# Two-layer hybrid decoder trunk: a table load, weight copies, turns and the last row's factors in another order

## The chip, the cores and the metric

The kernel runs on one core of a Trainium2 chip. The metric is the time of one execution on the device, in microseconds (us). Five engines work side by side, each through its own instructions in order: TensorE (PE in the profile; its weight loads are PEld), VectorE (DVE), ScalarE (ACT), GpSimd (POOL) and SyncE (SP), which issues most DMA transfers. They wait for each other by semaphores.

## The reference

The input is 512 tokens of 1024 channels in fp32. Two layers each do `h = h + mixer(rms_norm(h))` and then `h = h + ffn(rms_norm(h))`; a last RMSNorm gives the output.

```
# layer 0: gated short convolution beside causal pooling
proj = xn @ w_in_even                        # 1024 -> 4 x 512: a_b, a_c, a_v, z
y_a  = a_b * causal_dwconv3(a_c * a_v, conv_a)
y_b  = (causal_pool(z) @ w_pool) * pool_scale
h    = h + concat(y_a, y_b) @ w_out_even
# layer 1: chunked spatial gating
u, v = split(gelu(xn @ w_in_odd))            # 1024 -> 2 x 1024
vn   = rms_norm(v, sgu_norm)                 # chunks of 128 positions
gate = tril(w_spatial) @ vn + b_spatial
h    = h + (u * gate) @ w_out_odd
# both layers
g    = causal_dwconv3(hn @ w_gate, conv_ffn) + b_conv
h    = h + (silu(g) * (hn @ w_up)) @ w_down  # 2816 hidden
```

## The kernel before

The program is written in the order of the data: `mixer0`, `ffn0`, `mixer1`, `ffn1`. A scheduler then orders each engine's instructions by its own estimate, unless the text holds them in program order (`inorder`) or puts one behind another (`behind`). Activations are kept transposed, as eight tiles `h0` to `h7` of 128 channels by 512 tokens, up to the last projection.

**Precision.** A product in fp32 is made of three TensorE matmuls, on a high and a low part of each operand (`mm3`, L152). The high part is a ScalarE copy (`whi`, `hgh`, `a_hi`). The low part is a VectorE difference (`wlo`, `hgl`, `a_lo`), or, in `summed` (L135), a negated copy to which a DMA of GpSimd's queue adds the raw weight. Weights come through four buffers of 512 KB (`raw`), loaded on SyncE's queue; a load waits until the readers of the buffer's last content are done.

**Banks.** `mm_bank` hands out seven PSUM banks. A bank is free again when its reader (a copy, an addition) is done.

**Products by seven.** The feed-forward blocks, the v and u halves of mixer 1 and the last projection multiply 2 x 2 blocks by seven products in place of eight. The products use three kinds of banks (`BANK`, L529): products 1, 6, 7 and 4 all use bank "a" in turn, 5 and 3 use "e", 2 uses "b". So the copy of product 1 out of its bank goes before product 6, and the copy of 6 before 7.

**Norms.** A norm's factor is a root on ScalarE, which needs the table of its function loaded (`ACT_TABLE_LOAD`), a reciprocal and two corrections on VectorE (`newton`, L236). In mixer 0 the root is `sd_m0c`, the first root of the program; the copies of the input weights `ac` stand behind it on ScalarE.

**Feed-forward.** `steps` (L787) goes through 22 hidden tiles by groups: group 0 directly, groups 2, 4, ... by the seven products. `STEPS` (L522) tells for each group which half projection follows it and whether the rows it made are split into acts (`a_hi`, `a_lo`) behind it. `direct` (L604) runs group 0 of a feed-forward block: eight steps `i` of four sums `j` (`gu`), each step three matmuls per sum. In layer 1 a hook, `before` (L1097), puts a turn ahead of each of the first eight of these: `turn_residual` turns the residual by four TensorE transposes into a bank (`hT`), which ScalarE copies to `y`. On ScalarE the splits `t23` and `t41` of `block_sums` (L634) stand among these copies.

**Mixer 1.** `InProducts` (L896) holds one half of the input projection: `plain` makes the weights of products 1 and 2, `rest` the other five, in the order 5, 6, 7, 4, 3, and `run` the products, for two halves of the tokens (`i`). For v, `v1` is made by `plain`, `rest` and `run`. For u, `u0` is made by `plain`; then come the sums of squares of v, their root (`rv`), the normed v of the first half (`v_normed(0)`), then `rest` and `run`.

**The end.** The last projection runs product by product, with its order held by hand. For a row tile t, `taken` adds a product to `y`, `squared` makes a sum of squares, `halved` adds it up, `rooted` takes the root, `inverted` makes the factor in three VectorE instructions, `times` multiplies by the norm's gain, and `scaled` multiplies by the factor and issues the store. Row tile 3 ends before row tile 1, whose last sum comes in two parts, `c` and `d`.

Of the kernel before, what the change touches and what calls it, by code (L numbers as in the profile page):

```python
# [8 lines left out]
F32 = mybir.dt.float32  # L9
F32R = mybir.dt.float32r  # L10
BF16 = mybir.dt.bfloat16
AF = mybir.ActivationFunctionType
ALU = mybir.AluOpType
PSUM = bass.MemoryType.PSUM

P = 128
# [3 lines left out]
NT = S // P  # L20
# [7 lines left out]
LINE = 64  # L28
# [3 lines left out]
def tile_trunk(ctx: ExitStack, tc: tile.TileContext, x, norm_mix, norm_ffn, final_norm,  # L32
# [3 lines left out]
    nc = tc.nc  # L36
# [5 lines left out]
    tp = ctx.enter_context(tc.tile_pool(name="tp", bufs=2))  # L42
# [3 lines left out]
    def mm_bank(name):  # L46
        return ps_mm.tile([P, 512], F32, tag="mm", name=name)
# [40 lines left out]

    eps = small[:, 1:2]
    nc.gpsimd.memset(eps, EPS)  # L90
    inv_pos = small[:, PAD : 2 * PAD]
    for t in range(PAD):
        nc.gpsimd.memset(inv_pos[:, t : t + 1], 1.0 / (t + 1))
# [151 lines left out]
    def inv_sqrt(r, ss, n, name):  # L245

        ms = work("ms", n, name)
        nc.vector.tensor_scalar(ms, ss, 1.0 / D, EPS, op0=ALU.mult, op1=ALU.add)
        newton(ms, n, name, r)
        nc.vector.scalar_tensor_tensor(r, ms, 1.5, r, op0=ALU.add, op1=ALU.mult)  # L250

    def inv_sqrt_cols(ss, n, name):
        r = tp.tile([P, LINE], F32, tag="rc", name=f"rc_{name}")[:, :n]
        inv_sqrt(r, ss, n, name)
        return r
# [263 lines left out]

    STEPS = [(0, None, True), (2, (0, 2, 0), True), (4, (0, 2, 1), True)]  # L522
    for f in range(6, NF, 4):
        STEPS += [(f, (f - 4, f, 0), False), (f + 2, (f - 4, f, 1), f + 4 < NF)]
    HALF = S // 2
# [27 lines left out]
    class Ffn:  # L553
# [233 lines left out]
        def steps(self, half_down, before=lambda i, j: None):  # L787

            rows = []
            for f, part, ready in STEPS:  # L790
                rows += self.hidden(f, before)
# [29 lines left out]
    def mixer1(norm):  # L821
        w = w_in_odd[0]
        with tc.tile_pool(name="m1", bufs=1) as mp:
# [28 lines left out]
            ssv = mp.tile([P, 4, PAD], F32, name="ssv")[:, :, :NT]  # L852

            def v_square(half, t):
                sq = tp.tile([P, S], F32, tag="sq", name=f"sqv{half}_{t}")
                nc.scalar.activation(sq, v[t][:, half * 512 : (half + 1) * 512], AF.Square,
                                     accum_out=ssv[:, half, t : t + 1])
# [38 lines left out]
            class InProducts:  # L896
# [28 lines left out]
                    self.put(4, parts, (1, 0))  # L925
                    self.put(3, parts, (1, 1))

                def run(self, out_, done):
                    banks = ({}, {})
                    e = {}  # L930
                    for i, product in ((0, 1), (1, 1), (0, 2), (1, 2), (0, 6), (1, 6), (0, 5),
                                       (0, 7), (1, 5), (1, 7), (0, 4), (0, 3), (1, 4), (1, 3)):
                        hi, lo = self.stat[product]
                        ps = multiply(banks[i], f"{self.name}_{i}", product, tokens(product, i),
                                      lambda kp: (hi[:, kp, :], lo[:, kp, :]))
                        c = {1: (0, 0), 2: (0, 0), 6: (0, 1), 3: (0, 1), 7: (1, 1), 5: (1, 1),
                             4: (1, 0)}[product]
                        dst = out_(i + 2 * c[0])[:, c[1] * HALF : (c[1] + 1) * HALF]
                        if product in (1, 6):
                            nc.scalar.copy(dst, ps)  # L940
                        elif product == 5:
                            e[i] = ps
                        elif product == 7:
                            nc.scalar.copy(dst, ps)
                            nc.vector.tensor_tensor(dst, e[i], dst, ALU.add)
                            gelu(dst, dst, i + 2)
                        elif product == 4:
                            gelu(dst, ps, i + 2)
                            done(i + 2)
                        else:  # L950
                            nc.vector.tensor_tensor(dst, ps, dst, ALU.add)
                        if product == 3:
                            row = out_(i)
                            gelu(row, row, i)
                            done(i)

            def gelu(dst, src, t):
                nc.scalar.activation(dst, src, AF.Gelu, scale=norm.cols[:, t : t + 1])
# [3 lines left out]
            v = [mp.tile([P, D], F32, tag="v", bufs=4, name=f"v{t}") for t in range(NT)]  # L962
# [2 lines left out]
                v_square(0, t)  # L965
            v1 = InProducts("v1", 1536)
            v1.plain()
            v1.rest()
            v1.run(lambda t: v[t][:, 512:], lambda t: v_square(1, t))
            u0 = InProducts("u0", 0)  # L970
            u0.plain()

            nc.vector.tensor_tensor(ssv[:, 0, :], ssv[:, 0, :], ssv[:, 1, :], ALU.add)
            rv = inv_sqrt_cols(ssv[:, 0, :], NT, "v")
            vn = []

            def v_normed(half):
                hi = mp.tile([P, NT, S], F32R, tag="vn", bufs=4, name=f"vnh{half}")
                lo = mp.tile([P, NT, S], F32R, tag="vn", bufs=4, name=f"vnl{half}")
                for t in range(NT):  # L980
                    src = v[t][:, half * 512 : (half + 1) * 512]
                    nc.scalar.activation(hi[:, t, :], src, AF.Copy, scale=rv[:, t : t + 1])
                    nc.vector.scalar_tensor_tensor(lo[:, t, :], src, rv[:, t : t + 1],
                                                   hi[:, t, :].bitcast(F32),
                                                   op0=ALU.mult, op1=ALU.subtract)
                vn.append((hi, lo))

            v_normed(0)

            u, gt, mix = {}, {}, {}  # L990

# [32 lines left out]
                mix[j] = hi, lo  # L1024

            u[0] = mp.tile([P, NT, S], F32, tag="u", bufs=2, name="u0")
            u0.rest()
            u0.run(lambda t: u[0][:, t, :], lambda t: None)

            v_normed(1)  # L1030
            ws = wp.tile([P, NK, P], F32, tag="raw", bufs=4, name="ws")
            nc.scalar.dma_start(ws, w_spatial[0].rearrange("h t s -> t h s"))
# [46 lines left out]
    def ffn1(norm):  # L1079
        with tc.tile_pool(name="f1", bufs=1) as ap:  # L1080
# [9 lines left out]
            def turn_residual(t, half):  # L1090
                ps = mm_bank(f"hT{t}_{half}")
                for i in range(4):
                    nc.tensor.transpose(ps[:, i * P : (i + 1) * P],
                                        h[half * 4 + i][:, t * P : (t + 1) * P], ident)
                nc.scalar.copy(y[t][:, half * 512 : (half + 1) * 512], ps)

            def before(i, j):  # L1097
                if i < 2:
                    turn_residual(j, i)

            left, right = slice(0, 512), slice(512, D)

# [106 lines left out]
            vec, act, pool = nc.vector, nc.scalar, nc.gpsimd  # L1209
# [9 lines left out]
            def squared(t, cs):  # L1219
                sq = tp.tile([P, S], F32, tag="sq", name=f"sqf{t}_{cs.start}")  # L1220
                inorder(act.activation(sq[:, : cs.stop - cs.start], y[t][:, cs], AF.Square,
                                       accum_out=ssf[:, t, cs.start // 256 : cs.start // 256 + 1]))

            def halved(t, cs, first):

                ss, ms = ssf[:, t, cs.start // 256 : cs.start // 256 + 1], ssf[:, t, 3:4]
                inorder(vec.tensor_scalar(ms, ss, -0.5 / D, -0.5 * EPS if first else ms,
                                          op0=ALU.mult, op1=ALU.add))

            def rooted(t):  # L1230
                inorder(act.activation(root[t], ssf[:, t, 3:4], AF.Sqrt, scale=-2.0))

            def inverted(t):
                ms, r = ssf[:, t, 3:4], factor[t]
                inorder(vec.reciprocal(r, root[t]))
                inorder(vec.tensor_scalar(ms, ms, r, r, op0=ALU.mult, op1=ALU.mult))
                inorder(vec.tensor_scalar(r, ms, 1.5, r, op0=ALU.add, op1=ALU.mult))
# [4 lines left out]
            def scaled(engine, t, cs, queue=nc.sync):  # L1242
                dst, src, r = y[t][:, cs], rows_f[t][:, cs], factor[t]
                inorder(act.activation(dst, src, AF.Copy, scale=r) if engine is act else
                        engine.tensor_scalar(dst, src, r, None, op0=ALU.mult))
                queue.dma_start(out[t * P : (t + 1) * P, cs], dst)
# [43 lines left out]
            squared(1, right)  # L1290

            taken(2, 1, slice(0, 256), "c")
            inverted(3)
            taken(2, 1, slice(256, 512), "d")
            squared(1, left)
            halved(1, right, True)
            scaled(vec, 3, left)
            scaled(pool, 3, right)
            halved(1, left, False)
            rooted(1)  # L1300
            inverted(1)
            scaled(act, 1, right, nc.scalar)
            inorder(vec.scalar_tensor_tensor(y[1][:, left], y[1][:, left], factor[1],
# [37 lines left out]
```

## Time and profile before

| | us |
|---|---|
| three runs | 988.18, 988.68, 987.76 (median 988.18) |
| the profiled execution, own time | 987.73 |
| its span, first to last instruction | 986.0 |
| mean granted TensorE clock in it | 0.998 of full |

A row of the timeline gives the start (us from the span's start), the duration, the engine, the line, the operation, the tiles as out<-in (buffer numbers left out) and their shapes, and xN where N equal ones follow each other; in that case the duration is from the first's start to the last's end. In brackets stands how long the engine was idle before it, and what released it. Matmuls overlap: the next starts before the one before it has ended, and their ends are modelled.

### The profile page before, as it was taken

What the parts mean: (1) busy time and instruction counts of PE and PEld (TensorE: products, weight loads), DVE (VectorE), ACT (ScalarE), POOL (GpSimd) and SP (SyncE); (2) the same over time, 40 slices, a digit from 0 to 9 for tenths busy, and PEclk for the clock granted to TensorE, in tenths of its full rate; (3) what the DMA queues carried; (4) which work ended last, traced back from release to release, by engine and by line L of the source; (5) the groups of instructions that cost most, each with busy time, mean ns of one, the idle gap of its engine ahead of it and who ended that gap; (6) DMA issues with size and microseconds to landing.
All of it is one profiled execution on the core that took longest, in us unless ns stands there. A gap on an engine that the chain in (4) does not pass through costs nothing.

```text
span 986.0 us, 15484 instructions
## 1 busy us (share of the span) xinstructions
PE 974.6 (99%) x6099; PEld 879.9 (89%) x6099; DVE 772.8 (78%) x1179; ACT 560.8 (57%) x840; POOL 115.1 (12%) x131
## 2 busy tenths in 40 slices
PE   9999999999999999999999999999999999999996
PEld 6788888999999999999889988889999999999995
DVE  6897458998788887886887765579987779777787
ACT  5623347755465654655487734576655456554675
POOL 2142022000000000000210001210000000000023
PEclk9999999999999999999999999999999999999999
DMA  7442225555565454643423623165554555455674
GB/s 248 131 150 85 86 86 128 137 143 150 129 151 135 130 142 129 150 129 109 127 63 113 196 78 104 54 142 129 150 160 132 137 136 146 127 132 145 151 151 126
DMA packets 87941, 129.32 MB, mean 131 GB/s; under 512 B 4308, under 2 KB 57788, under 8 KB 87868
## 3 DMA queue, kind: packets, MB, share of 16 engines
q1 hardware_dynamic: 78172, 98.69, 32.3%
q0 software_dynamic: 8208, 27.79, 15.6%
q10 hardware_dynamic: 1488, 1.84, 0.7%
q8 instruction: 48, 0.79, 0.3%
q14 instruction: 25, 0.20, 0.1%
HBM read 98.42 MB, written 2.10 MB: 102 GB/s over the span
## 4 chain that ended last, share of the span: by engine, by line
PE 86%; DVE 7%; ACT 3%; issue 2%; DMA 1%; POOL 0%; ACTq 0%; DVEq 0%
PE dn L154 3%; PE dn L153 3%; PE dn L155 3%; PE d L154 3%; PE d L153 3%; PE d L155 3%; PE oo L155 1%; PE oo L154 1%; PE oo L153 1%; PE oe L155 1%; PE oe L154 1%; PE oe L153 1%; PE u_20a L542 1%; PE u_16a L542 1%; PE u_14a L542 1%
## 5 line engine op out<-in xcount | busy, mean ns | idle before, releaser
L576 DVE SCALAR_TENSOR_TENSOR c<-rows,prm,c 128x512 f32<-128x512 f32 x88 | 64.0, 745 | 1.5 <-ACT c L574 1.4
L140 POOL DMA_DIRECT2D wlo_g<-raw_g x20 | 17.2, 859 | 387.4 <-ACT wlo_g L139 350.4
L153 PE MATMUL d<-a_hi,whi_d 128*128 128x512 f32 x144 | 56.1, 390 | 0.0
L153 PE MATMUL dn<-whi_dn,a_hi 128*128 128x512 f32 x144 | 56.1, 390 | 0.0
L154 PE MATMUL d<-a_lo,whi_d 128*128 128x512 f32 x144 | 56.1, 390 | 0.0
L154 PE MATMUL dn<-wlo_dn,a_hi 128*128 128x512 f32 x144 | 56.1, 390 | 0.0
L155 PE MATMUL d<-a_hi,wlo_d 128*128 128x512 f32 x144 | 56.0, 389 | 0.0
L155 PE MATMUL dn<-whi_dn,a_lo 128*128 128x512 f32 x144 | 56.0, 389 | 0.0
L679 DVE TENSOR_TENSOR wlo_s34u<-s34u,whi_s34u 128x1024 fp32r<-128x1024 f32 x20 | 24.5, 1224 | 25.5 <-ACT whi_s34u L678 25.5
L149 DVE TENSOR_TENSOR wlo_dn<-raw_dn,whi_dn 128x1024 fp32r<-128x1024 f32 x18 | 22.0, 1224 | 23.6 <-ACT whi_dn L148 23.4
L142 ACT ACTIVATE whi_u<-raw_u 128x1024 fp32r<-128x1024 f32 x21 | 22.2, 1055 | 31.7 <-PE d L154 17.6
L149 DVE TENSOR_TENSOR wlo_d<-raw_d,whi_d 128x1024 fp32r<-128x1024 f32 x18 | 22.0, 1223 | 19.5 <-ACT whi_d L148 19.5
L198 ACT ACTIVATE hgh<-h,prm 128x512 fp32r<-128x512 f32 x24 | 17.3, 722 | 35.1 <-DVE h L309 35.0
L140 POOL DMA_DIRECT2D wlo_u<-raw_u x21 | 18.1, 861 | 162.0 <-ACT wlo_u L139 89.5
L584 ACT ACTIVATE s<-c,prm 128x512 f32<-128x512 f32 x44 | 31.2, 713 | 7.3 <-DVE c L576 7.2
L209 POOL TENSOR_TENSOR ssq_f<-ssq_f,sq_f 128x512 f32<-128x512 f32 x14 | 19.7, 1410 | 131.2 <-ACT sq_f L208 96.3
L260 ACT ACTIVATE a_hi<-s 128x512 fp32r<-128x512 f32 x40 | 25.0, 626 | 15.7 <-PE dn L154 9.9
L199 DVE SCALAR_TENSOR_TENSOR hgl<-h,prm,hgh 128x512 fp32r<-128x512 f32 x24 | 23.1, 964 | 12.0 <-ACT hgh L198 11.9
L155 PEld LDWEIGHTS d<-a_hi,wlo_d 128*128 128x128 f32 x144 | 27.0, 188 | 5.7
L155 PEld LDWEIGHTS dn<-whi_dn,a_lo 128*128 128x128 f32 x144 | 27.0, 188 | 5.6
L1104 DVE SCALAR_TENSOR_TENSOR y<-dn,small,y 128x512 f32<-128x512 f32 x40 | 27.7, 746 | 5.5 <-PE dn L155 5.5
L153 PEld LDWEIGHTS d<-a_hi,whi_d 128*128 128x128 f32 x144 | 27.1, 188 | 5.4
(1489 smaller groups left out, 3759.2 us busy)
## 6 DMA issues: line engine op xcount, KB each, us to landing
raw_g<-in_w_ffn_gate_dram SPq DMA_DIRECT2D x40, 512.0 KB, 3.8
raw_u<-in_w_ffn_up_dram SPq DMA_DIRECT2D x40, 512.0 KB, 3.7
raw_dn<-in_w_ffn_down_dram SPq DMA_DIRECT2D x22, 512.0 KB, 3.5
wlo_u<-raw_u POOLq DMA_DIRECT2D x21, 512.0 KB, 5.6
wlo_g<-raw_g POOLq DMA_DIRECT2D x20, 512.0 KB, 4.6
raw_d<-in_w_ffn_down_dram SPq DMA_DIRECT2D x18, 512.0 KB, 3.8
raw_oe<-in_w_out_even_dram SPq DMA_DIRECT2D x8, 512.0 KB, 3.5
raw_v<-in_w_in_odd_dram SPq DMA_DIRECT2D x8, 512.0 KB, 4.7
```

Source lines behind the costliest of these rows:

```text
L140: nc.gpsimd.dma_start(lo, raw, accum_op=ALU.add)
L149: behind(nc.vector.tensor_tensor(lo, raw, hi.bitcast(F32), ALU.subtract), after[0])
L153: nc.tensor.matmul(ps, lhs[0], rhs[0], start=start, stop=False)
L154: nc.tensor.matmul(ps, lhs[0], rhs[1], start=False, stop=False)
L155: nc.tensor.matmul(ps, lhs[1], rhs[0], start=False, stop=stop)
L199: nc.vector.scalar_tensor_tensor(hg[k][1], h[k], g, hg[k][0].bitcast(F32), op0=ALU.mult, op1=ALU.subtract)
L260: nc.scalar.activation(hi, src, AF.Copy, scale=scale)
L542: nc.tensor.matmul(ps, l, r, start=first, stop=end, skip_group_check=True)
L576: nc.vector.scalar_tensor_tensor(c, t[:, i : S + i], prm("cf", i * NF + ft), c, op0=ALU.mult, op1=ALU.add)
L584: nc.scalar.activation(s, c, AF.Silu, bias=self.prm("bf", ft))
L679: nc.vector.tensor_tensor(lo, src, hi.bitcast(F32), ALU.subtract)
L1104: return nc.vector.scalar_tensor_tensor(dst, ps, ffn.cols[:, t : t + 1], dst, op0=ALU.mult, op1=ALU.add)
```

## The change

Six edits. `sd_0` is a one-element root, issued at the program's start. `STEPS` no longer splits the rows of group 2 behind group 2; they are split together with those of group 4 (both layers). `run` takes a function that it calls behind the two products 1, ahead of product 2: for v1 that is `rest`; for u0 it is a new `beside_u0`, with the root of v, the first normed v and `rest`, which stood ahead of `run`. `before` issues the turns two at a time, ahead of every second sum. At the end, row 3's factor stands behind the last sum and its square; its right half is scaled by VectorE in place of GpSimd, behind the root of row 1.

```diff
     nc.gpsimd.memset(eps, EPS)
+    nc.scalar.activation(tp.tile([P, LINE], F32, tag="sd", bufs=1, name="sd_0")[:, :1], eps, AF.Sqrt)
...
-    STEPS = [(0, None, True), (2, (0, 2, 0), True), (4, (0, 2, 1), True)]
+    STEPS = [(0, None, True), (2, (0, 2, 0), False), (4, (0, 2, 1), True)]
...
-                def run(self, out_, done):
+                def run(self, out_, done, behind_first):
...
                     for i, product in ((0, 1), (1, 1), (0, 2), (1, 2), (0, 6), (1, 6), (0, 5),
                                        (0, 7), (1, 5), (1, 7), (0, 4), (0, 3), (1, 4), (1, 3)):
+                        if (i, product) == (0, 2):
+                            behind_first()
...
-            v1.rest()
-            v1.run(lambda t: v[t][:, 512:], lambda t: v_square(1, t))
+            v1.run(lambda t: v[t][:, 512:], lambda t: v_square(1, t), v1.rest)
             u0 = InProducts("u0", 0)
             u0.plain()
-            nc.vector.tensor_tensor(ssv[:, 0, :], ssv[:, 0, :], ssv[:, 1, :], ALU.add)
-            rv = inv_sqrt_cols(ssv[:, 0, :], NT, "v")
...
-            v_normed(0)
...
-            u0.rest()
-            u0.run(lambda t: u[0][:, t, :], lambda t: None)
+
+            def beside_u0():
+                nc.vector.tensor_tensor(ssv[:, 0, :], ssv[:, 0, :], ssv[:, 1, :], ALU.add)
+                rv.append(inv_sqrt_cols(ssv[:, 0, :], NT, "v"))
+                v_normed(0)
+                u0.rest()
+
+            u0.run(lambda t: u[0][:, t, :], lambda t: None, beside_u0)
...
             def before(i, j):
-                if i < 2:
+                if i < 2 and j % 2 == 0:
                     turn_residual(j, i)
+                    turn_residual(j + 1, i)
...
             taken(2, 1, slice(0, 256), "c")
-            inverted(3)
             taken(2, 1, slice(256, 512), "d")
             squared(1, left)
+            inverted(3)
             halved(1, right, True)
             scaled(vec, 3, left)
-            scaled(pool, 3, right)
             halved(1, left, False)
             rooted(1)
+            scaled(vec, 3, right)
             inverted(1)
             scaled(act, 1, right, nc.scalar)
```

More of the change, by code (lines that the diff above doesn't have):

```diff
@@ L967, in mixer1 @@
             v1.plain()
-            v1.rest()
-            v1.run(lambda t: v[t][:, 512:], lambda t: v_square(1, t))
+            v1.run(lambda t: v[t][:, 512:], lambda t: v_square(1, t), v1.rest)
             u0 = InProducts("u0", 0)
             u0.plain()
-            nc.vector.tensor_tensor(ssv[:, 0, :], ssv[:, 0, :], ssv[:, 1, :], ALU.add)
-            rv = inv_sqrt_cols(ssv[:, 0, :], NT, "v")
-            vn = []
+            vn, rv = [], []
             def v_normed(half):
@@ L981, in v_normed @@
                     src = v[t][:, half * 512 : (half + 1) * 512]
-                    nc.scalar.activation(hi[:, t, :], src, AF.Copy, scale=rv[:, t : t + 1])
-                    nc.vector.scalar_tensor_tensor(lo[:, t, :], src, rv[:, t : t + 1],
+                    nc.scalar.activation(hi[:, t, :], src, AF.Copy, scale=rv[0][:, t : t + 1])
+                    nc.vector.scalar_tensor_tensor(lo[:, t, :], src, rv[0][:, t : t + 1],
                                                    hi[:, t, :].bitcast(F32),
```

## The prediction

> **What bounds the kernel now.** I read the page's busy times first, then the chain that ended last, then the timeline at every place where TensorE starts a matmul later than its stream allows.
>
> ```profile
> PE 974.6 (99%) x6099; PEld 879.9 (89%) x6099; DVE 772.8 (78%) x1179; ACT 560.8 (57%) x840; POOL 115.1 (12%) x131
> ...
> PE 86%; DVE 7%; ACT 3%; issue 2%; DMA 1%; POOL 0%; ACTq 0%; DVEq 0%
> ```
>
> TensorE is busy for 99% and carries 86% of the chain. No matmul is added or removed, so only its stalls and the stretch behind its last matmul can move. Busy time hides stalls, since the ends are modelled; they are read from starts.
>
> ```profile
> 199.69 1.28 DVE L262 TENSOR_TENSOR a_lo<-s,a_hi 128x512 fp32r<-128x512 f32 x2
> 200.90 1.21 DVE L679 TENSOR_TENSOR wlo_s12u<-s12u,whi_s12u 128x1024 fp32r<-128x1024 f32 x1
> 200.92 0.40 PE L542 MATMUL u_4e<-t,whi_s12u 128*128 128x256 f32 x2
> 202.16 0.39 PE L542 MATMUL u_4e<-t,wlo_s12u 128*128 128x256 f32 x1 [0.25 <-DVE wlo_s12u L679]
> 202.39 0.40 PE L542 MATMUL u_4e<-t,whi_s12u 128*128 128x256 f32 x2
> ...
> 977.32 0.28 PE L1204 MATMUL dn_d<-whi_dnp,hgl 128*128 128x256 f32 x1
> ```
>
> One 256-column matmul shows 0.28 us and two show 0.40, so they start 0.12 apart. A stall therefore costs the idle time in brackets plus 0.16 of overlap: 0.25 + 0.16 = 0.41. The matmul behind it starts 0.23 later instead of 0.12, so every stall costs 0.11 more. I book 0.52 here.
>
> **Second group's acts later (-0.52).** The stall waits for wlo_s12u, which ends at 202.11 behind two a_lo splits that begin 1.21 before it. As the changed program is built, both stand behind the two s34u differences, so wlo_s12u runs from 199.69 to 200.90. TensorE's order there also changes: the first matmul with wlo_s12u now comes third, and is wanted at 200.92 + 2 x 0.12 = 201.16, so 0.26 is left. Nobody needs acts 2 and 3 before the half projection behind group 6, some 20 us on. The s34u differences come 1.2 sooner, and with them the buffers that SyncE's next two loads wait for; only the two splits come later. In layer 1 the trace has no such stall, so I book nothing there. Bounds: 0 (VectorE not ahead after all) and 0.52.
>
> **Root's table first (-0.21).**
>
> ```profile
> 5.34 0.63 ACT L394 ACTIVATE whi_z<-raw_z 128x512 fp32r<-128x512 f32 x1 [2.60 <-DMA raw_z<-in_w_in_even_dram]
> ...
> 31.74 1.28 ACT L240 ACT_TABLE_LOAD   x1
> 33.14 1.04 ACT L148 ACTIVATE whi_ac<-raw_ac 128x1024 fp32r<-128x1024 f32 x1
> ...
> 32.28 0.16 DVE L248 TENSOR_SCALAR ms_m0c<-ssc_m 128x4 f32<-128x4 f32 x1 [3.30 <-PE ssc_m L226]
> 33.96 0.27 DVE L111 COPY prm<-prm_ps 128x112 f32<-128x112 f32 x1
> 34.22 1.23 DVE L149 TENSOR_TENSOR wlo_ac<-raw_ac,whi_ac 128x1024 fp32r<-128x1024 f32 x1
> ...
> 33.57 0.26 PE L109 MATMUL prm_ps<-ident,pk 112*128 112x112 f32 x1
> 34.24 0.50 PE L153 MATMUL ac<-hgh,whi_ac 128*128 128x512 f32 x1 [0.41 <-ACT whi_ac L148]
> 35.73 0.85 PE L155 MATMUL ac<-hgh,wlo_ac 128*128 128x512 f32 x3
> ```
>
> The built program has one table load less ahead of mixer 0's root: the load at the start now brings the root's set, and behind it stands the added one-column activation. Both lie in the 2.60 that ScalarE idles for its first data, so they cost nothing; without that cover the added one would cost a few tenths at the start. The root then waits for ms_m0c, over at 32.44, and no longer for the table, over at 33.02. So whi_ac starts 0.57 earlier and the first ac matmul could go at 34.24 - 0.57 = 33.67. But what is late next is wlo_ac. It stands behind the copy of prm, which needs prm_ps, over at 33.83 on TensorE. So the copy moves from 33.96 to 33.87 only, and wlo_ac to 34.13, over at 35.36. The matmuls that want it could come at 35.73 - 0.57 = 35.16 and get it at 35.42, which is 0.31 better than now, and this new stall brings its 0.11: 0.20 is left, 0.21 unrounded. Bounds: 0, and the whole 0.57.
>
> **Mixer 1, v (-0.50).**
>
> ```profile
> 517.49 2.96 ACT L148 ACTIVATE whi_v<-raw_v 128x1024 fp32r<-128x1024 f32 x3
> 520.33 0.38 ACT L940 COPY v<-v_0a 128x256 f32<-128x256 f32 x1
> ...
> 520.76 0.39 PE L542 MATMUL v_0a<-whi_v,s 128*128 128x256 f32 x1 [0.23 <-ACT v L940]
> ...
> 526.79 1.23 DVE L918 TENSOR_TENSOR raw_u<-raw_u,raw_u 128x1024 f32<-128x1024 f32 x1 [2.91 <-DMA raw_u<-in_w_in_odd_dram]
> ```
>
> (Times in both mixer 1 parts leave out the savings before them, which move every engine alike.) Product 6 reuses product 1's bank, whose copy to SBUF stood behind three weight copies. Now it goes first, at 517.49, so the whole stall goes: 0.23 + 0.16 + 0.11 = 0.50. What the copies overtake gets later: weight 7 by one copy (0.25), weights 4 and 3 by two copies or by one of them and an addition that VectorE now does in between (up to 0.6). TensorE comes to product 7 only 36 matmuls after 520.4, at 524.7. But these splits free the buffers of u0's four loads on SyncE's queue, and L918, the first difference of u0's weights, is a wait for one of them: it slips by x, between 0.23 (the loads stream behind each other, so the first one's delay counts) and 0.6. I take 0.4.
>
> **Mixer 1, u0 (-0.58).**
>
> ```profile
> 540.60 1.28 ACT L240 ACT_TABLE_LOAD   x1
> 542.01 0.35 ACT L940 COPY u<-u_0a 128x256 f32<-128x256 f32 x1
> 543.36 2.56 ACT L982 ACTIVATE vnh<-v,rc_v 128x512 fp32r<-128x512 f32 x4 [0.72 <-DVE rc_v L250]
> 545.83 0.35 ACT L940 COPY u<-u_0a 128x256 f32<-128x256 f32 x1
> ...
> 542.42 0.39 PE L542 MATMUL u_0a<-whi_u,s 128*128 128x256 f32 x1 [0.40 <-ACT u L940]
> ```
>
> The same kind of stall: 0.40 + 0.16 + 0.11 = 0.67 that the copy's new place, ahead of weight copies 4 and 3 and of the root, takes away. What is queued behind these on ScalarE is the normed v (four activations), and behind it the copy of product 6, which product 7 waits for. In the built order the table load of the root loses weight copy 3 ahead of it (0.96, by the three in 2.96 above) and gains the two copies (0.25 to 0.35 each): it comes 0.3 to 0.5 sooner, plus x. The normed v follows the table's end by the root's chain, 1.48 now, at most 0.2 less: 542.7 to 543.0, plus x. The copy ends 2.47 + 0.35 behind that, at 545.5 to 545.8 plus 0.4. TensorE, without the seven u_0e matmuls that stood ahead and without both stalls, starts product 6 at 542.42 - 0.56 - 0.84 - 0.50 = 540.52 and wants product 7's bank 45 matmuls on, at 545.92. The two touch; I book 0.09 back. Bounds: 0.67 saved, and 0.1 saved with x = 0.6 and all else at its later end (a wait of 0.5, and its 0.11).
>
> **Turns by twos (+0.51).**
>
> ```profile
> 595.28 1.03 PE L1020 MATMUL mT<-ident,gt 128*128 128x128 f32 x8
> 596.07 0.48 PE L153 MATMUL oo<-mx,whi_oo 128*128 128x512 f32 x1
> 596.39 0.40 PE L154 MATMUL oo<-mx,whi_oo 128*128 128x512 f32 x1
> ...
> 631.54 0.60 PE L1093 MATMUL hT<-ident,h 128*128 128x128 f32 x4
> 633.81 0.60 PE L1093 MATMUL hT<-ident,h 128*128 128x128 f32 x4
> 639.44 0.60 PE L1093 MATMUL hT<-ident,h 128*128 128x128 f32 x4
> ...
> 637.61 0.63 ACT L654 ACTIVATE t<-t 128x512 fp32r<-128x512 f32 x1 [0.71 <-DVE t L645]
> 638.66 0.57 ACT L1095 COPY y<-hT 128x512 f32<-128x512 f32 x1
> ```
>
> Two turns with their six matmuls take 633.81 - 631.54 = 2.27 now. Eight transposes in a row are in the trace: 0.79, then 0.32, then five matmuls at 0.227 (three in 0.85 above less one of 0.40): 2.25. Pairing itself saves 0.02 a pair. But each second turn comes 1.1 sooner and wants a bank by then. Four of the seven banks hold the sums, three are left for turned tiles, and as built the eighth turn takes the bank of the fifth, now as before. ScalarE copies the fifth from 638.66 to 639.23, behind two splits of t41 that wait for VectorE's L645; in the new order the same two stand ahead of it (a third split, of t23, runs before that wait ends). Now the eighth turn starts at 639.44 and never notices. Paired, it is wanted at 631.54 + 3 x 2.25 + 0.35 = 638.64 and gets its bank at 639.28. From there 0.35 of transposes, 0.32 and five times 0.227 end at 641.08, against 639.44 + 1.13 = 640.57 now. Bounds: -0.05 with no wait, +0.62 with the usual 0.11.
>
> The Trainium skill, "TensorE: Matmul & The Clock Gate", section "LDWEIGHTS (loading the stationary operand)", has a weight load last as long as its columns need at 1.2 GHz, about 107 ns for 128. By it eight transposes, one load each, would take 0.85, not 0.79, and the stretch would be 0.25 longer in all; it speaks against pairing, and the trace agrees but for 0.06 a run of eight.
>
> **The end (-0.34).**
>
> ```profile
> 977.11 0.48 DVE L1104 SCALAR_TENSOR_TENSOR y<-dn_c,small,y 128x256 f32<-128x256 f32 x1
> 978.13 0.47 DVE L1104 SCALAR_TENSOR_TENSOR y<-dn_d,small,y 128x256 f32<-128x256 f32 x1
> 978.58 0.48 DVE L1245 TENSOR_SCALAR y<-yf,ssf 128x512 f32<-128x512 f32 x1
> 978.70 0.63 ACT L1221 ACTIVATE sqf<-y 128x512 f32<-128x512 f32 x1 [0.66 <-DVE ssf L1227]
> 979.46 0.21 DVE L1227 TENSOR_SCALAR ssf<-ssf 128x1 f32<-128x1 f32 x1 [0.40 <-ACT sqf L1221]
> 979.94 0.16 DVE L1235 RECIPROCAL ssf<-ssf 128x1 f32<-128x1 f32 x1 [0.27 <-ACT ssf L1231]
> ```
>
> The last matmul ends at 977.60, yet dn_d is taken at 978.13, behind row 3's factor. With the factor behind it, it starts at 977.64 (0.49 earlier), and so does the square, 978.21. On VectorE the same pieces stand between dn_c and the left scaling, in another order, plus the 0.14 that dn_d now waits for its matmul (it could start at 977.50): the left scaling moves from 978.58 to 978.72, and lets the sum (979.46 now) start at 979.12, since such an operation overlaps the next by 0.08. ScalarE's half of the sum is there at 978.97. So the sum is 0.34 earlier. The right scaling, taken from GpSimd, is 0.48 like its left twin, and fills the gap of 979.46 to 979.94 in which VectorE waits for the root; its store leaves SyncE's queue before the last one comes. Everything up to the last stores follows by 0.34. Without that gap the right scaling would cost 0.40. Bounds: 0.14 (it overhangs by 0.2) and 0.49.
>
> **Sum.** -0.52 - 0.21 - 0.50 - 0.58 + 0.51 - 0.34 = -1.64 on an execution whose own time is 987.73 (span 986.0 and 1.7 around it). The median of the runs is 988.18, 0.45 above; I lay the same 1.64 on it: 986.5, or 0.17% less. That is inside the 0.2% (1.98 us) that I take as what a measurement of this kernel can tell from no change.
>
> **Rivals.** *The turns find their bank.* If the fifth copy comes 0.64 earlier, the pairing costs nothing: -2.2, 986.0. For it: the stall hangs on one ScalarE copy. Against: that copy and the two splits ahead of it keep their order, and the wait on VectorE behind L645 stays. *Mixer 1 gives back.* With x = 1, product 7 waits 0.7 and 0.11 more, which takes back all of u0's part and a bit: 986.5 + 0.8 = 987.3. For it: the margin is nil in my sum. Against: the loads follow one another, so their delay stays near the first one's 0.23. *The load train decides.* The loads of u0 could lose their place by several us, since SyncE issues them as VectorE frees buffers and L918 already waits for one 2.91. Then the whole queue of ScalarE behind it, root, normed v and copy, slips and TensorE with it, us for us: from x = 1.9 the kernel is slower than before; at x = 3 product 7 waits 2.7 and the time is 989.3. Against it stands that only 0.6 of delay is visible at its source.
>
> **Chances and numbers.** Forecast 0.60 (own range 985.9 to 987.0), free turns 0.20, giving back 0.14, load train 0.06. Time 986.5. The range goes down to 985.4, free turns (986.0) with the upper bounds of table, u0 and end (0.36, 0.09, 0.15 more), and up to 988.0, giving back (987.3) with the lower bounds of table and end and half of the second group's gain gone (0.21, 0.20, 0.26). Faster by over 0.2% (below 986.2): 0.20 from free turns and a quarter of the forecast's 0.60, so 0.35. Slower by over 0.2% (above 990.2): the load train with x over 3.9, and what I do not see, 0.05. The rest is 0.60.
>
> **What would show it.** In the changed profile: no idle before u_4e with wlo_s12u, before the second v_0a and the second u_0a; a table load before the first data and none before mixer 0's root; a short idle at the first ac matmuls that take wlo_ac; a wait of about 0.6 for ScalarE's copy before the last turn; dn_d taken within 0.05 of its last matmul, the last stores issued 0.34 nearer to it. Wrong would be: turns without a wait, an idle of several tenths before u0's product 7, or new stalls among groups 4 to 8, where VectorE's order changed too and I found nothing late.

## The result and the profile after

| | before | changed |
|---|---|---|
| median of 15 runs each | 987.86 | 986.02 |
| lowest and highest | 986.82, 988.97 | 985.17, 987.48 |
| profiled execution, own time | 987.73 | 985.52 |
| its span | 986.0 | 983.8 |

The ratio of the runs is 0.9982, with a 95% interval of 0.9974 to 0.9990: 1.84 us less, or between 1.0 and 2.6. The two profiled executions differ by 2.21. The forecast was 986.5, by a sum of -1.64.

The page of the changed kernel has TensorE as nearly the whole chain of waits; the shares of ScalarE, issue and DMA, 6% together before, are gone from it, and VectorE's fell from 7% to 1%.

```profile
PE 95%; DVE 1%; ACT 0%; issue 0%; ACTq 0%
```

The view of waits lists what TensorE stood idle for: who waited, on whom, us in all, how often, the longest. From 30 us on (to 960 before, to 980 after), first before, then changed:

```profile
PE ac L153 <- ACT whi_ac L148: 0.4, 1, 0.4
PE u_0a L542 <- ACT u L940: 0.4, 1, 0.4
PE u_4e L542 <- DVE wlo_s12u L679: 0.2, 1, 0.2
PE v_0a L542 <- ACT v L940: 0.2, 1, 0.2
```

```profile
PE hT L1097 <- ACT y L1099: 0.3, 1, 0.3
```

Four waits went and one came, the eighth turn's. The timeline of the changed kernel, place by place, in the order of the program:

```profile
35.35 0.98 PE L156 MATMUL ac<-hgh,wlo_ac 128*128 128x512 f32 x3
...
200.69 0.40 PE L543 MATMUL u_4e<-t,whi_s12u 128*128 128x256 f32 x2
200.93 0.28 PE L543 MATMUL u_4e<-t,wlo_s12u 128*128 128x256 f32 x1
...
539.69 0.28 PE L543 MATMUL u_1b<-whi_u,hgl 128*128 128x256 f32 x1
539.81 0.28 PE L543 MATMUL u_0a<-whi_u,s 128*128 128x256 f32 x1
...
636.46 0.60 PE L1097 MATMUL hT<-ident,h 128*128 128x128 f32 x4
637.37 0.66 PE L1097 MATMUL hT<-ident,h 128*128 128x128 f32 x4 [0.31 <-ACT y L1099]
...
661.18 0.28 PE L543 MATMUL g_2e<-t,wlo_s12g 128*128 128x256 f32 x1
661.30 0.40 PE L543 MATMUL g_2a<-t,whi_s12g 128*128 128x256 f32 x2
...
975.72 0.28 PE L1209 MATMUL dn_d<-whi_dnp,hgl 128*128 128x256 f32 x1
```

At 200.93 and 539.81 a matmul follows the one before it by the regular 0.12 where a stall stood, and so does product 6 of v at 519.65. At 35.35 is the short new stall that the forecast named. At 637.37 the eighth turn starts 0.91 behind the seventh, where four transposes take 0.35 if a matmul of another kind follows, and 0.44 if more transposes do (they start 0.11 apart). And at 661.30 the first g_2a follows by 0.12. Before, it came 0.28 behind its neighbour, 0.16 more than the regular, and the next pair 0.10 late behind it; the forecast had nothing to say on that. The timeline before has ScalarE's copy there, and the idle on the row of the weight load:

```profile
662.39 0.35 ACT L736 COPY rows<-g_2a 128x256 f32<-128x256 f32 x1
...
662.80 0.30 PEld L542 LDWEIGHTS g_2a<-t,whi_s12g 128*128 128x128 f32 x2 [0.20 <-ACT rows L736]
```

Read from the starts of TensorE's matmuls, the shifts against before are, place by place: -0.24 for the table, -0.49 for the second group, -0.49 and -0.64 in mixer 1, +0.51 at the turns, -0.25 at g_2a. The last matmul starts 1.60 sooner (975.72 against 977.32).

The other 0.6 lies behind the last matmul. Timeline of the end, changed kernel:

```profile
974.83 3.79 SPq L1251 DMA_DIRECT2D out_dram<-y  x3
...
976.04 0.48 DVE L1109 SCALAR_TENSOR_TENSOR y<-dn_d,small,y 128x256 f32<-128x256 f32 x1
...
976.94 0.21 DVE L1242 TENSOR_SCALAR ssf<-ssf 128x1 f32<-128x1 f32 x1
977.07 0.14 DVE L1232 TENSOR_SCALAR ssf<-ssf 128x1 f32<-128x1 f32 x1
...
977.26 0.48 DVE L1250 TENSOR_SCALAR y<-yf,ssf 128x512 f32<-128x512 f32 x1
977.66 0.21 DVE L1232 TENSOR_SCALAR ssf<-ssf 128x1 f32<-128x1 f32 x1
...
979.71 0.33 SPq L1310 DMA_DIRECT2D out_dram<-y  x1
```

and of the kernel before, its stores alone:

```profile
976.43 4.91 SPq L1246 DMA_DIRECT2D out_dram<-y  x3
...
981.48 0.36 SPq L1305 DMA_DIRECT2D out_dram<-y  x1
```

dn_d is taken 0.32 behind the start of its last matmul, as forecast. The sum (977.66) comes 1.94 behind it, against 2.14 before: 0.20 sooner, not 0.34. SyncE's last store is issued 3.99 behind it, against 4.16: 0.17. But the span ends 8.1 behind it, against 8.7. One part of the difference is in the stores: before, the third of SyncE's last three ended its issue at 981.34, 0.14 ahead of the final one; now at 978.62, 1.1 ahead. The DMA view shows what that does, GB/s in 40 slices, before from 980 to 986 (0.15 each), then changed from 977.5 to 983.8 (0.16 each):

```profile
GB/s 0 0 0 0 0 0 0 0 0 300 423 355 369 383 369 341 410 410 383 355 382 382 423 328 369 383 423 191 14 55 0 0 0 0 0 0 0 0 0 0
```

```profile
GB/s 0 0 0 0 0 0 13 325 403 364 416 377 403 338 403 273 65 0 0 234 377 390 325 364 377 377 403 338 78 26 26 13 0 0 0 0 0 0 0 0
```

Before, four stores of 256 KB run through one after the other at about 380 GB/s, 2.8 us; now two and two, with a gap between them. The other part is in GpSimd's last instruction; the experiments on the end, below, tell the two apart.

### The profile page after: what moved, and what is told of

It is laid out like the page before. It is cut to its first block, busy times and chain, and to the rows that moved or that the text cites. A ratio compares the mean times of both kernels' runs of the same rounds, so it can differ in the third digit from the quotient of the medians.

```text
span 983.8 us, 15476 instructions
## 1 busy us (share of the span) xinstructions
PE 973.4 (99%) x6099; PEld 879.5 (89%) x6099; DVE 774.2 (79%) x1180; ACT 560.1 (57%) x840; POOL 112.6 (11%) x130
## 3 DMA queue, kind: packets, MB, share of 16 engines
q10 hardware_dynamic: 1488, 1.84, 0.6%
## 4 chain that ended last, share of the span: by engine, by line
PE 95%; DVE 1%; ACT 0%; issue 0%; ACTq 0%
PE dn L155 3%; PE d L154 3%; PE dn L154 3%; PE d L155 3%; PE d L156 3%; PE dn L156 3%; PE oe L156 1%; PE oe L155 1%; PE oe L154 1%; PE oo L156 1%; PE oo L155 1%; PE oo L154 1%; PE gu L154 1%; PE gu L156 1%; PE gu L155 1%; PE u_20a L543 1%
## 5 line engine op out<-in xcount | busy, mean ns | idle before, releaser
L154 PEld LDWEIGHTS dn<-whi_dn,a_hi 128*128 128x128 f32 x144 | 27.1, 188 | 5.4
```

Source lines behind the costliest of these rows:

```text
L154: nc.tensor.matmul(ps, lhs[0], rhs[0], start=start, stop=False)
```

## The experiments

Starts differ between executions: the first ssc_m matmul of mixer 0 came between 30.68 and 31.80 in the twelve profiled executions of this study. So where the last matmul is compared below, it is taken from that start (the stretch: 977.32 - 31.19 = 946.13 before, 975.72 - 31.20 = 944.52 changed), and the end from the last matmul.

**The second group's acts alone.**

```diff
-    STEPS = [(0, None, True), (2, (0, 2, 0), True), (4, (0, 2, 1), True)]
+    STEPS = [(0, None, True), (2, (0, 2, 0), False), (4, (0, 2, 1), True)]
```

> The kernel before with the second group's acts split later, nothing else. Theory: the 0.41 stall at 202.16 and the 0.11 behind it go, and nothing else on TensorE changes, so its last matmul starts 0.52 sooner, at 976.80 in place of 977.32; the stall at 662.80 (0.16 and 0.10) stays, since it comes from ScalarE's order around the turns. Rival: the splits that leave VectorE in layer 1 take that stall away too: last matmul at 976.54.

The stall at 202 is gone, 0.50 with what stood behind it; at 662.00 g_2a still stalls, for 0.12 and 0.10. So the acts do not explain that second saving. The stretch is 945.08, which is 1.05 less than before, not 0.52: the other half is the stall ahead of u0's product 6, which was 0.66 in the profile before and is 0.13 here, though nothing there was edited. The same stall was 0.34, 0.33, 0.39 and 0.13 in four other kernels that leave u0 as it was. The timeline of acts alone, with product 6 of v, L918 and product 6 of u0 (the rows of before stand in the prediction):

```profile
520.54 0.39 PE L542 MATMUL v_0a<-whi_v,s 128*128 128x256 f32 x1 [0.24 <-ACT v L940]
...
526.02 1.23 DVE L918 TENSOR_TENSOR raw_u<-raw_u,raw_u 128x1024 f32<-128x1024 f32 x1 [2.37 <-DMA raw_u<-in_w_in_odd_dram]
...
541.65 0.39 PE L542 MATMUL u_0a<-whi_u,s 128*128 128x256 f32 x1
```

| | L918 behind v_0a | u_0a behind v_0a | stall |
|---|---|---|---|
| before | 6.03 | 21.66 | 0.66 |
| end, engine only | 5.76 | 21.38 | 0.39 |
| turns alone | 5.72 | 21.34 | 0.34 |
| end alone | 5.71 | 21.33 | 0.33 |
| acts alone | 5.48 | 21.11 | 0.13 |
| end, order only | 5.40 | 21.13 | 0.13 |

From 5.7 on the stall grows with L918 us for us (0.33 later, 0.33 more), and L918 waits for a load of u0's weights. The size of this term is that of the load's landing in one execution; the mean of the six is 0.33.

**The turns alone, and all but the turns.**

```diff
-                if i < 2:
+                if i < 2 and j % 2 == 0:
                     turn_residual(j, i)
+                    turn_residual(j + 1, i)
```

> The kernel before with the turns by twos, nothing else. Theory: the eighth turn waits about 0.5 for ScalarE's copy of the fifth and TensorE is 0.51 later behind the turns; but the new order of ScalarE's splits brings its sums and weight copies sooner and takes the stall at 662.80 (0.26) away, so the last matmul starts at 977.32 + 0.51 - 0.26 = 977.57. Rival (as forecast): the stall at 662.80 has another cause and stays: 977.83. Rival: the eighth turn's wait needs the other parts: 977.3 or less.

> The changed kernel with the turns one by one as before. Theory: the wait of 0.61 goes, turns cost 0.10 more otherwise, and the stall at 662.80 comes back with 0.26: last matmul at 975.72 - 0.51 + 0.26 = 975.47, own time 985.3. Rival: that stall went by the other parts: 975.21, own time 985.0. Rival: the wait is made up later, and nothing is gained: 975.7.

Turns alone, the eighth turn and the last matmul:

```profile
639.25 0.66 PE L1093 MATMUL hT<-ident,h 128*128 128x128 f32 x4 [0.32 <-ACT y L1095]
...
977.61 0.28 PE L1205 MATMUL dn_d<-whi_dnp,hgl 128*128 128x256 f32 x1
```

All but the turns, at g_2a and the last matmul:

```profile
660.95 0.51 PE L543 MATMUL g_2a<-t,whi_s12g 128*128 128x256 f32 x2
...
975.47 0.28 PE L1208 MATMUL dn_d<-whi_dnp,hgl 128*128 128x256 f32 x1
```

The wait appears with the turns alone, and the stall at g_2a is gone there; without them the wait is gone and the stall is back (660.95 is 0.27 behind its neighbour), at 975.47 as expected. Own time 985.03. The stretch with the turns alone equals that of before to 0.01, with u0's stall 0.32 shorter: the turns cost 0.51, give 0.25 back at g_2a and cost 0.26 net, beside small change of 0.06. The giving back is not TensorE's doing. As built, the new order brings the last of ScalarE's block sums (`t<-h,prm`, at 644.26 in the changed kernel, at 648.08 before) ahead of its weight copy `wlo_g`, and what follows moves up: the copy `whi_s12u` starts 2.7 sooner (655.60 for 658.31), where TensorE is 1.3 sooner. In the changed kernel the copy `rows<-g_2a` (L737) starts at 659.69 and TensorE's g_2a at 661.30, where before only 0.41 lay between the two. That the order of the turns takes the stall away is shown by these runs; which of ScalarE's moves does it was read from the timelines, not tried by itself.

**Three pairs, then one by one.** The first six turns stay in pairs.

```diff
-                if i < 2 and j % 2 == 0:
+                if (i, j) in ((0, 0), (0, 2), (1, 0)):
                     turn_residual(j, i)
                     turn_residual(j + 1, i)
+                elif (i, j) in ((1, 2), (1, 3)):
+                    turn_residual(j, i)
```

> The changed kernel with the first six turns by twos and the last two one by one. Theory: ScalarE's order of splits, sums and copies stays the early one, so the stall at 662.80 stays away; the eighth turn comes three matmuls later and finds its bank, so the 0.61 in front of it is gone: last matmul at 975.72 - 0.61 + 0.02 = 975.13, median 985.4, ratio to before 0.9975. Rival: the stall at 662.80 comes back (0.26): 975.4 and 985.7. Rival: the eighth turn still waits: no faster than the changed kernel, ratio 0.998.

Median 985.40 over 10 runs, against 987.67 for the kernel before in the same session: ratio 0.9978 (0.9969 to 0.9987). Turns seven and eight:

```profile
636.81 0.60 PE L1097 MATMUL hT<-ident,h 128*128 128x128 f32 x4
...
637.93 0.60 PE L1097 MATMUL hT<-ident,h 128*128 128x128 f32 x4
```

No wait at the eighth turn, none at g_2a: the stretch is 944.01, 0.51 less than the changed kernel's. The last matmul itself, 975.58, missed the expected 975.13 mainly because this execution's ssc_m began 0.37 later.

**The parameters earlier.** On top of three pairs:

```diff
             def ahead(k):
+                nonlocal prm0
                 if k + 1 < NK:
                     turn(k + 1)
+                if k == 5:
+                    prm0 = params0()
...
-            prm0 = params0()
```

> As the one before, and the parameters of layer 0 are turned and copied behind input tile 6 in place of behind mixer 0's root. Theory: wlo_ac stands behind whi_ac alone, the stall at 35.35 (0.16 and 0.11) goes: last matmul at 974.86, median 985.2, ratio 0.9973. Rival: something else is late there (the weights that are loaded behind parameters of layer 1): 975.1 or more.

A miss. The stall at wlo_ac went, and another came ahead of it: the transposes that spread mixer 0's factor stand earlier in TensorE's built order and wait for that factor.

```profile
33.96 0.40 PE L156 MATMUL z<-hgh,wlo_z 128*128 128x512 f32 x1
34.18 0.16 DVE L251 SCALAR_TENSOR_TENSOR rc_m0c<-ms_m0c,rc_m0c 128x4 f32<-128x4 f32 x1
...
34.49 0.51 PE L217 MATMUL ssr_m<-ident,rc_m0c 128*128 128x128 f32 x3
```

The stretch is 943.92, only 0.09 less than with three pairs alone; median 985.33, ratio 0.9976 (0.9967 to 0.9985), which the intervals do not tell apart from three pairs. What is late next at that place is the root's chain on VectorE.

**The end: alone, its order alone, its engine alone.** Order alone keeps `scaled(pool, 3, right)`; engine alone keeps `inverted(3)` where it was:

```diff
-            inverted(3)
             taken(2, 1, slice(256, 512), "d")
             squared(1, left)
+            inverted(3)
```

```diff
             scaled(vec, 3, left)
-            scaled(pool, 3, right)
             halved(1, left, False)
             rooted(1)
+            scaled(vec, 3, right)
```

> The kernel before with the new end, nothing else. Theory: last matmul unchanged at 977.32; the last two stores are issued 0.17 sooner (981.31 and 981.36); behind them the last packet ends some 2.74 later in place of 2.85, because the stores of row 3 are out of the way, and the program closes 0.3 sooner after it; own time 987.1. Rival: all beyond the 0.17 is chance between two executions: own time 987.55. Rival (as forecast): the sum, and with it the last stores, come 0.34 sooner, at 981.14.

> The kernel before with the end's new order, but the right half of row 3 still scaled by GpSimd. Theory: the sum comes 0.2 sooner, but GpSimd's half starts 0.5 later than before and its store leaves SyncE's queue only some 3.7 behind the start of the last matmul, with the left half's and row 1's store queued behind it, so the last store is issued 4.5 behind that start (4.16 before) and the stores follow each other as before: own time 0.3 above before. Rival: the gain is all in the order, and the last store comes at 3.95, own time about that of the whole new end.

> The kernel before with the right half of row 3 scaled by VectorE behind the root of row 1, and the factor of row 3 where it was, ahead of the last sum. Theory: the last store is issued 4.2 behind the start of the last matmul (4.16 before), but it no longer stands behind two stores of row 3, so the span ends about 3.9 behind the last issue in place of 4.5: own time some 0.6 below before. Rival: the ends of the stores differ by chance only: 4.5 behind the last issue, own time as before.

Order alone: SyncE's last four issues, the last matmul, and row 3's right half on GpSimd:

```profile
976.87 4.71 SPq L1246 DMA_DIRECT2D out_dram<-y  x3
...
977.76 0.28 PE L1204 MATMUL dn_d<-whi_dnp,hgl 128*128 128x256 f32 x1
...
979.41 1.82 POOL L1245 TENSOR_SCALAR y<-yf,ssf 128x512 f32<-128x512 f32 x1 [0.31 <-ACT sqf L1221]
...
981.71 0.35 SPq L1305 DMA_DIRECT2D out_dram<-y  x1
```

Engine alone:

```profile
977.59 0.28 PE L1204 MATMUL dn_d<-whi_dnp,hgl 128*128 128x256 f32 x1
...
979.37 1.33 SPq L1246 DMA_DIRECT2D out_dram<-y  x2
...
981.79 0.33 SPq L1305 DMA_DIRECT2D out_dram<-y  x1
```

Each engine closes its program with a `DRAIN`. GpSimd's stands in the list of the closing line (L1337, in the changed kernel L1342), with the duration in ns (least, median, most) and the start; order alone first, then before, then changed:

```profile
L1337 POOLq DRAIN  x1: 6607/6607/6607, 979.4 to 979.4; - x1
```

```profile
L1337 POOLq DRAIN  x1: 6862/6862/6862, 978.4 to 978.4; - x1
```

```profile
L1342 POOLq DRAIN  x1: 6214/6214/6214, 975.6 to 975.6; - x1
```

Its record starts ahead of GpSimd's last computing instruction, and in all twelve kernels it ends 4.74 behind the end of that instruction.

| from the start of the last matmul | SyncE's last store issued | SyncE has seen all stores land (its own DRAIN ends) | GpSimd's DRAIN ends | span ends |
|---|---|---|---|---|
| before | 4.16 | 7.72 | 7.93 | 8.70 |
| acts alone | 4.16 | 8.28 | 7.86 | 9.03 |
| turns alone | 4.16 | 8.14 | 7.93 | 8.89 |
| u0 alone | 4.16 | 7.59 | 7.86 | 8.63 |
| order alone | 3.95 | 7.29 | 8.21 | 8.98 |
| engine alone | 4.20 | 7.30 | 6.06 | 8.05 |
| end alone | 3.99 | 7.09 | 6.07 | 7.85 |
| changed | 3.99 | 7.34 | 6.08 | 8.09 |
| new end in four more kernels | 3.98 to 3.99 | 7.08 to 7.09 | 6.06 to 6.08 | 7.83 to 7.85 |

In every row the span ends 0.75 to 0.77 behind the later of the two columns before it. The order brings the last issue forward by 0.2 and has the stores landed 0.3 to 1.0 sooner than in the four kernels with the old end, although GpSimd's half, whose issue ends 0.13 ahead of the last one (976.87 + 4.71, against 981.71), is still among them. But the span ends no sooner: GpSimd's half now runs later, so its DRAIN ends at 8.21, 0.92 after SyncE has seen the stores land. The engine leaves the issue where it was; it takes the DRAIN out of the way and has the stores landed 0.3 to 1.0 sooner as well. Order alone and end alone differ by the engine only: of the 1.13 between their ends, 0.2 is the stores and 0.92 the DRAIN. For order alone the theory was wrong on the issue (its rival had 3.95 right). The end it gave, 0.3 above before, did come (8.98 against 8.70), but by luck: the DRAIN sets it, not the stores that the theory had follow each other. That run's own time (988.45) also holds an idle of 0.28 at 964, from VectorE's order as built there; it lies ahead of the last matmul and so is not in the table. End alone measured 986.22, better than its expected 987.1, with a start 0.5 earlier than before's and u0's stall at 0.33.

**u0 alone.** `run` calls `beside_u0` behind the products 1 of u0 (the root of v and the first normed v move with it), v1 as before.

```diff
-            u0.rest()
-            u0.run(lambda t: u[0][:, t, :], lambda t: None)
+            u0.run(lambda t: u[0][:, t, :], lambda t: None, beside_u0)
```

> The kernel before with mixer 1's u0 part alone. Theory: the stall ahead of product 6 of u0, which was 0.1 to 0.66 in six kernels with the old order as the load behind L918 landed 5.4 to 6.0 behind the start of product 6 of v, goes whatever that load does: no gap over 0.05 from 530 to 555; ScalarE's chain follows L918, which v's part does not delay here, so product 7 finds its bank with a margin of about 0.5 to 1.0. The stalls at 202, 520 and 662 stay. Rival: product 7 waits: a gap at about 547.

No stall ahead of product 6, none ahead of product 7. The copy that product 7 needs, in the first row, is over at 545.74, 1.05 ahead of it; in the changed kernel (second fence) at 544.65, 0.56 ahead:

```profile
545.39 0.35 ACT L942 COPY u<-u_0a 128x256 f32<-128x256 f32 x1
...
546.79 0.28 PE L542 MATMUL u_0a<-whi_u,s 128*128 128x256 f32 x1
```

```profile
525.92 1.23 DVE L919 TENSOR_TENSOR raw_u<-raw_u,raw_u 128x1024 f32<-128x1024 f32 x1 [2.48 <-DMA raw_u<-in_w_in_odd_dram]
...
544.30 0.35 ACT L943 COPY u<-u_0a 128x256 f32<-128x256 f32 x1
...
545.21 0.28 PE L543 MATMUL u_0a<-whi_u,s 128*128 128x256 f32 x1
```

TensorE is 0.49 later without v's part, and the margin 0.49 wider: ScalarE's chain goes by the load, not by TensorE, and v's part spends half of the room that u0's part has.

**The normed v late.** Three more activations ahead of it, on the kernel with all but the turns:

```diff
+                for n in range(3):
+                    sq = tp.tile([P, S], F32, tag="sq", name=f"late{n}")
+                    nc.scalar.activation(sq, v[3][:, :512], AF.Copy, scale=rv[0][:, 3:4])
                 v_normed(0)
```

> The kernel of no_turns with three more 128x512 activations ahead of the first normed v (copies that nobody reads). In the built order TensorE puts all twelve u_1e matmuls ahead of product 7 of u0, three more (0.36) than in no_turns. Theory: what holds product 7 is ScalarE's copy of product 6 behind the normed v, with a margin of 0.51 in no_turns (copy over at 544.62, product 7 at 545.19, 0.06 between a copy and its matmul): three times 0.62 less 0.51 and 0.36 leave a stall of 0.98, with 0.11 behind it, and the last matmul starts at 975.47 + 1.09 = 976.56. Rival (the forecast's reading, margin nil): 977.07. Rival: another thing holds product 7 and the delay is hidden: 975.5.

```profile
545.29 0.28 PE L543 MATMUL u_1e<-whi_u,s 128*128 128x256 f32 x1
546.40 0.39 PE L543 MATMUL u_0a<-whi_u,s 128*128 128x256 f32 x1 [0.83 <-ACT u L943]
546.62 0.28 PE L543 MATMUL u_0a<-wlo_u,s 128*128 128x256 f32 x1
```

546.40 is 1.11 behind its neighbour in place of 0.12, a stall of 0.99, and the next matmul comes 0.22 behind it in place of 0.12: 1.09 in all. The stretch grows from 944.26 to 945.32, by 1.06. So it is this copy that product 7 waits for, and the margin of half a us in the combined kernel is real. The rival with no margin would have cost 1.60.

## Why the prediction was right, and where its terms were off

The time fell where it was forecast, and the likeliest case was the one that came: the turns cost, the rest saves. By the prediction's own steps, with what the profiled execution shows:

| step | forecast | measured | |
|---|---|---|---|
| second group's acts later | -0.52 | -0.49 | right, stall and the 0.11 behind it |
| root's table first | -0.21 | -0.24 | right, with the new stall at wlo_ac |
| mixer 1, v | -0.50 | -0.49 | right |
| mixer 1, u0 | -0.58 | -0.64 | size by chance: the stall is 0.33 in the mean of six kernels |
| turns by twos | +0.51 | +0.51 | right, but it also gives 0.25 back |
| g_2a in layer 1 | 0 | -0.25 | not forecast |
| the end | -0.34 | -0.6 | 0.17 by the forecast's own path, the rest unpriced: 0.9 over all kernels (7.9 for 8.8 in the mean) |
| sum | -1.64 | -2.2 | |

*The stalls of one engine's order* (acts, v, the first of the two in mixer 0) were read from one timeline and were right to 0.03. The table and v's part were not run alone; their terms are read at their places in the changed kernel, where the stalls that they were to remove are gone. The rule of the prediction that a stall costs its idle time, the overlap it interrupts and 0.11 more held up in those read here, also in the stall that was made on purpose.

*The turns.* The price of the wait was right for the reason given: the fifth copy on ScalarE, behind t41's splits. The rival in which the turns find their bank fell by the run with the turns alone. A pair costs what the prediction took: the changed kernel's first eight transposes start at 629.68 and their successor at 630.47, which is 0.79, as in mixer 1. From the Trainium skill, "TensorE: Matmul & The Clock Gate", section "LDWEIGHTS (loading the stationary operand)", the estimate is 0.85 for the eight weight loads. The trace comes nearer to that than the prediction says: the eight start 0.11 apart, the successor only 0.03 behind the last, and the matmul behind it 0.09 late, so that the eight cost 0.88 in all. By the same count the seventh turn takes 0.44 and not 0.35, and the eighth waits about 0.5, not 0.64; the sum did not suffer, since the bank's release sets the time. What the step missed: it followed ScalarE's new order as far as that copy ("in the new order the same two stand ahead of it") and no further. The trace of before had a stall at 662.80 that hung on a copy of ScalarE's, and an edit that reorders ScalarE can take such a stall away as well as make one.

*Mixer 1, u0.* The two inputs that were off are the stall's size and x. The stall of 0.67 was booked as a constant, though the prediction itself had found that L918, a wait for a load, sets ScalarE's chain; six executions show 0.13 to 0.66. And x, booked at 0.4, is -0.14 against the profile before (525.92, where 526.79 less the 0.73 saved ahead of it is 526.06); against the kernels with L918 at 5.7 behind v_0a it is about 0.2, the low bound of the prediction. So product 7 has a margin of 0.56, not of nothing, and neither "mixer 1 gives back" nor "the load train decides" came near. For the latter, only the slope is shown: us for us, once the margin is gone. That the term came out at -0.64 for -0.58 is chance: the profile before has the largest of the six stalls.

*The end.* Its sum was to come 0.34 sooner and came 0.20 sooner. 0.13 of the 0.14 that is missing went where the prediction took the same pieces in another order to cost the same: the left scaling now stands close behind its own factor (L1242, 976.94 to 977.15). It starts 0.19 behind the small sum ahead of it (977.07), where before, with dn_d in between, it was 0.06. The two runs agree: 0.19 with the order alone, 0.06 with the engine alone. Another 0.03 to 0.05 is the right scaling's overhang, so the last issue gains 0.17. The larger error is that everything behind the last issue was taken to follow it ("Everything up to the last stores follows by 0.34"). Two things there had no price. With GpSimd's half out of the burst of stores, SyncE sees them all landed 0.38 sooner in the changed kernel (7.34 for 7.72), 0.17 of which is the issue. And before, the span waited another 0.21 for GpSimd's DRAIN, which the change takes out of the way by giving the half to VectorE.

*The sum and the runs.* With the typical size of u0's term (0.33 for 0.64) and of the end (0.9 for 0.6), the measured terms give 2.2 again; the medians say 1.84, within an interval of 1.0 to 2.6. The forecast's 1.64 lies in it partly by luck: two terms that it did not have, at g_2a and behind the last issue, more than make up for a stall at u0 that is smaller in most executions than the one it read. More than that these runs don't resolve: three pairs, 0.5 faster in the stretch than the changed kernel, measured 985.40 in another session, and the two were not timed side by side.

## What to carry to other kernels

Read a stall's size off more than one execution where its releaser hangs on a load: its place is firm, its size is not. When a scheduler rebuilds an order, ask of every stall that exists whether it survives, not only where a new one may arise. And at the end of a kernel follow the chain beyond the last store's issue: to the landing of the stores, which is later when more of them are issued together, and to the closing instruction of every engine. An engine that is off the critical path can still be the last to close.

## What the runs showed of the hardware

GpSimd's closing DRAIN ended 4.74 us behind the end of GpSimd's last computing instruction in all twelve kernels, and the span ended 0.75 to 0.77 behind the later of that and SyncE's having seen the stores land. In three kernels, before among them, the DRAIN was the later one, with the order alone by 0.92. Four stores of 256 KB issued within about 1 us went through at about 380 GB/s one behind the other, for 2.8 us (before); with the engine alone, where two of them are issued over 1 us ahead, the stores had landed 0.42 sooner behind about the same issue (7.30 and 7.72). And the same matmul of mixer 0 comes up to 1.1 us apart between executions (30.68 to 31.80), so that single times of kernels that differ by less say little; what sets that start was not looked into.
